# Adjacent columns for the stationary operands of the widest attention pattern, in a float32 decoder step on one core

## Chip, core and metric

The kernel runs on one core of a Trainium2 chip. The metric is the device time of one execution in microseconds; the kernel before takes 2777.18 us (median of three runs, 2773.69 to 2778.02).

## What is computed

One step of a decoder layer for a prompt of 2048 tokens and 8 sample tokens, width 1024, all in float32: a norm, one input projection to q, k, v and u, dilated attention on q, k, v (8 heads of 64) beside pooling on u, an output projection, an MLP with 4096 hidden features, a gated per-layer input and a final norm. The attention has three patterns, whose outputs are merged by their softmax denominators:

```python
DILATION_PATTERNS = ((128, 1), (512, 4), (2048, 16))
def _dilated_attn_prompt(q, k, v, window, dil):
    span = window // dil
    ...   # tokens are regrouped by residue modulo dil; in a class a query sees its own row and span rows before
    s = jnp.einsum('bdhnqe,bdhnke->bdhnqk', qb, kb).astype(jnp.float32) * ATTN_SCALE
    mask = (rel >= 0) & (rel <= span) & (key_idx >= 0)
    s = jnp.where(mask, s, NEG_INF)
    m = jnp.max(s, axis=-1, keepdims=True)
    p = jnp.exp(s - m)
    den = jnp.sum(p, axis=-1)
    ...
def _mixer_out(outs, lses, pooled, w_out):
    wts = jax.nn.softmax(jnp.stack(lses, axis=0), axis=0)
    attn = jnp.einsum('gbth,gbthe->bthe', wts, jnp.stack(outs, axis=0))
    ...
    return jnp.concatenate([attn, pooled], axis=-1) @ w_out
```

In the widest pattern (dilation 16) each of the 16 classes of the prompt has 128 tokens.

## The kernel before

Every float32 factor is split into a high and a low part, and each product is the sum of three passes on TensorE (line 190 records all of them). The projections run as groups of 24 passes with a stationary weight tile of 128x128 and 264 to 512 token columns moving. They are the work in front; the attention is a generator of steps in the background, which `Pace` mixes into the groups in proportion to the columns passed (lines 1526 and 1546). A scheduler with its own model of the chip then orders each engine's queue, so an engine's order can differ from the order in which the code is written. Each engine takes its queue in order.

The attention runs twice: `Att(0)` (called A here, from about 228 to 640 us) for the queries of tokens 0 to 1023, beside the second half of the input projection and `ple_mm`; `Att(1)` (B, about 640 to 1535 us) for the others, beside the output projection and most of the MLP of the first tokens. The rest, from 1535 us on, has the sample's last part, the other tokens' projections, MLP and gates, and no prompt attention.

Tokens are stored by their residue modulo 4: `khl[:, r, c]` is the key of token 4c + r (high part in rows 0 to 63, low part below), `qhh[:, r, c]` the query's high part twice, `ql` its low part. The class of dilation 16 is every fourth column of one `r`, written `s::4`, a step of 16 bytes. Per head there are three parts:

- `prep` and `prep_v` load and split keys, queries and values.
- `maxima` (line 761) gets an upper bound of the scores from single passes with the queries stationary; VectorE reduces them (line 771). For each `r` come two products of the middle pattern and four of the widest (line 789), with stationary `qhh[:, r, s::4]` and moving keys with the same step: 64 of them in A, 128 in B. For the first pattern GpSimd copies the queries of four blocks into the buffer `qn` (line 796, 128x512), two copies per head and half, and each serves four products (line 807).
- `out` runs `units` (line 865): scores, exponentials (ScalarE), masks (GpSimd), split (ScalarE, VectorE), and one unit later the products with the values (`pv`, `pv_wide`). Units of the middle pattern for r, r+1, then one of the widest for both (line 908), twice per head, then the first pattern. The widest unit has 16 score products: for each of 2 r and 4 s one with stationary keys `khl[:, r, s::4]` and moving `qhh`, and one with stationary `k1` (a copy of the keys' upper half by ScalarE, line 898, with a row of ones) and moving `ql`. Stationary are 64 columns in A, 128 in B; moving are 64.

For the first pattern GpSimd copies keys into natural order into the ring `nat` of two buffers (line 932), ScalarE into `k1` (line 933). After the last head of A, `prep_cat` loads the attention's output from DRAM, multiplies it by the reciprocal denominators and splits it (VectorE, ScalarE); the output projection (`out_proj`) uses the tiles of the pooling first and the tile of the last two heads last.

```python
                    mm(o, qhh[:, r, s::4], khl[:, r, s : 4 * self.kp : 4], True, True)
                ...
                    scores(ps[:kp, E * u : E * u + E], khl[:, r, s : 4 * kp : 4], k1s[u // 4][:, s : 4 * kp : 4],
                           qhh[:, r, s::4], ql[:, r, s::4])
```

Of the kernel before, what the change touches and what calls it, by code (L numbers as in the profile page):

```python
# [12 lines left out]
ALU = mybir.AluOpType  # L13
# [4 lines left out]
P = 128  # L18
D = 1024            # model width
KD = D // P         # feature tiles of the model width  # L20
SEQ = 2048
NS = 8              # sample tokens
# [7 lines left out]
WIN = 2048          # rows of the key/value cache  # L30

# Token 512 n + 4 i + r lies at position 512 n + 128 r + i; the sample's tokens lie behind the prompt's.
# Chunks of positions (first, length), each a PSUM bank's worth: phase 1 in two halves ...
IN_PART = [[(0, 512), (512, 512)], [(1024, 384), (1408, 384), (1792, 264)]]
# ... and the later phases in two parts, the first of which needs no token behind the 1,024th.
# [5 lines left out]
# On-chip memory in 4-byte columns: split operands (float32r), float32 data, two blocks that change hands.  # L41
GRAIN = 2 * LC        # a split operand of a chunk
COLS_R = 41 * GRAIN
COLS_MA = 3400
# [4 lines left out]
class Arena:  # L49
    """Columns of a few buffers, handed out by the oldest free stretch that is long enough."""  # L50
# [49 lines left out]
class Region(Arena):  # L100
    """Stretches of an arena, handed out in their turn."""
# [14 lines left out]
class Ring:  # L116
    """n buffers used in turn."""
# [31 lines left out]
def decoder_step(ctx: ExitStack, tc: tile.TileContext, I, O):  # L149
# [59 lines left out]
    class Pace:  # L209
        """Background steps spread over the work in front (columns through the tensor engine)."""  # L210
# [16 lines left out]
    def mix(a, na, b, nb, lead=1.0):  # L227
        """steps of a and b in proportion, those of b sooner by the factor lead"""
        i = j = 0
        while i < na or j < nb:  # L230
            if j * na >= i * nb * lead and i < na or j >= nb:
                i += 1
                next(a, None)
            else:
                j += 1
                next(b, None)
            yield
        drain(a)
        drain(b)

# [31 lines left out]
    # mask2: query i (partition) against the previous and the own block in natural order.  # L272
    # mask1: query (r, i') against (r, previous 32 | own 32), tokens 4 i' + r.
    # mask3: query 64 + i against the keys of its class.
# [23 lines left out]
    def TINY(cols, rows=P, key="", n=7, width=16):  # L298
        """a narrow buffer, in turn with those of the same key"""
# [7 lines left out]
    def newton(out, v, scr1, scr2):  # L307
        """out = v ** -0.5 with one Newton step behind the square root and the reciprocal."""
# [18 lines left out]
    def load_w(src, nk, nf=P, wr=None, ring=None):  # L327
        """src: DRAM [nk * 128, nf] -> its two parts, each [P, nk, nf]."""
# [12 lines left out]
    def group(ps, ln, ws, xs, hook=None):  # L341
        """ps = sum over k of w[k].T x[k], in the passes that float32 accuracy asks for."""
# [9 lines left out]
    class Acts:  # L352
        """Split activations [k][chunk] -> [P, 2, length]."""
# [37 lines left out]
    def pieces(pos, ln):  # L391
        """(first, end, group, offset in the group) of the stretch of positions"""
# [8 lines left out]
    def prep_x(hf, xa, rg, tp):  # L401
        """rg: rings xl, xraw, junk; tp: banks for the transposes"""
# [129 lines left out]
    def pool_state(rg, tp):  # L532
        """the sums over the buffered rows in the windows of the sample's tokens"""
# [24 lines left out]
    def group_done(ft, n, t, rg, tp):  # L558
        """t: one feature tile of q, k, v or u for the 512 positions of group n"""
# [23 lines left out]
    def in_proj(hf, xa, order, rg, mp, tp, hook, ws, first=None):  # L583
        """first: steps that come beside the first chunk's products of the first two tiles, and ahead of the other chunk's"""
# [1084 lines left out]
```

## Time and profile before

| | us |
|---|---|
| median of three runs | 2777.18 |
| span of the profiled execution, first to last instruction | 2772.4 |
| TensorE busy in it | 2701.8 |
| VectorE busy | 1525.1 |
| GpSimd busy | 978.0 |
| ScalarE busy | 805.3 |

The profile has no other time for the profiled execution than its span. Matmuls are pipelined: a matmul's duration in a row covers its fill and drain and overlaps its neighbours', so rows of TensorE are best read by the starts of runs. The granted clock is 1.00 at full speed and 0.50 at half.

### The profile page before, as it was taken

How to read it: one execution, taken by the hardware profiler on the slowest of the kernel's cores; microseconds unless marked ns; L12 is line 12 of the kernel's file. 1: busy time of each engine (PE TensorE's matmuls, PEld its weight loads, DVE VectorE, ACT ScalarE, POOL GpSimd, SP SyncE). 2: the span in 40 equal slices, each digit the busy share in tenths (PEclk: the TensorE clock that was granted, in tenths of full speed). 3: DMA queues.
4: the chain of work that ended last, by engine and by line, in shares of the span. 5: the costliest groups of instructions: out<-in, count | busy, mean ns of one | idle time of the engine just before them, and what ended most of it. 6: DMA issues, size and time to landing. Idle time of an engine off the chain costs nothing. (4 is left out here: it accounts for less than half of the span.)

```text
span 2772.4 us, 42788 instructions
## 1 busy us (share of the span) xinstructions
PE 2701.8 (97%) x15686; PEld 2588.0 (93%) x15686; DVE 1525.1 (55%) x3303; ACT 805.3 (29%) x1541; POOL 978.0 (35%) x1270
## 2 busy tenths in 40 slices
PE   8999999999989999999999999999999999999998
PEld 6788899988989999999999899899999999999997
DVE  6737866666586665755655766532332332322675
ACT  5211344452423133242332424411011011011354
POOL 2414634422375333332432734412122122122263
PEclk9999999999999999999999999999999999999999
DMA  7464345467153232332321554431111111111124
GB/s 245 136 176 124 90 109 135 105 211 195 39 160 107 72 87 69 103 101 71 91 71 50 156 155 145 130 115 42 43 39 39 39 40 44 39 39 39 52 83 148
DMA packets 386192, 272.50 MB, mean 98 GB/s; under 512 B 91722, under 2 KB 349461, under 8 KB 385973
## 3 DMA queue, kind: packets, MB, share of 16 engines
q1 hardware_dynamic: 385397, 269.68, 34.1%
q8 instruction: 123, 2.02, 0.3%
q14 instruction: 88, 0.72, 0.1%
q0 software_dynamic: 512, 0.07, 0.0%
q10 hardware_dynamic: 72, 0.02, 0.0%
HBM read 209.47 MB, written 60.30 MB: 97 GB/s over the span
## 5 line engine op out<-in xcount | busy, mean ns | idle before, releaser
L190 PE MATMUL bank<-mem_r 128*128 128x416 f32 (+10 forms) x13544 | 2501.4, 342 | 36.2 <-DVE mem_r L196 10.6
L190 PEld LDWEIGHTS bank<-mem_r 128*128 128x128 f32 (+3 forms) x13544 | 2359.5, 189 | 108.9 <-DVE mem_r L196 16.6
L199 POOL TENSOR_SCALAR mem_r<-mem_f 128x512 fp32r<-128x512 f32 (+1 forms) x444 | 323.8, 734 | 852.3 <-PE bank L190 729.5
L196 DVE TENSOR_TENSOR mem_r<-mem_f,mem_r 128x512 fp32r<-128x512 f32 (+4 forms) x568 | 432.6, 767 | 217.8 <-POOL mem_r L199 161.8
L196 DVE TENSOR_TENSOR mem_f<-bank,mem_f 128x416 f32<-128x416 f32 (+3 forms) x488 | 273.1, 566 | 257.8 <-PE bank L190 251.2
L196 DVE TENSOR_TENSOR mem_r<-mem_mb,mem_r 128x416 fp32r<-128x416 f32 (+6 forms) x236 | 172.9, 739 | 363.9 <-ACT mem_r L1310 310.4
L1307 ACT ACTIVATE mem_mb<-bank 128x392 f32<-128x392 f32 (+1 forms) x160 | 82.4, 515 | 799.3 <-PE bank L190 797.9
L196 POOL TENSOR_TENSOR mem_mb<-mem_mb 128x416 f32<-128x416 f32 (+1 forms) x140 | 142.4, 1017 | 314.8 <-ACT mem_mb L1307 290.9
L771 DVE CUSTOM_DVE_ANT_0 bank<-bank,mask 128x256 f32<-128x256 f32 (+3 forms) x504 | 158.5, 340 | 32.9 <-PE bank L190 29.0
L196 DVE TENSOR_TENSOR mem_ma<-bank,mem_ma 128x416 f32<-128x416 f32 (+2 forms) x104 | 63.5, 610 | 84.5 <-PE bank L190 71.5
L1310 ACT CAST mem_r<-mem_mb 128x416 fp32r<-128x416 f32 (+1 forms) x128 | 68.5, 535 | 139.6 <-POOL mem_mb L196 139.5
L834 POOL TENSOR_SCALAR_AFFINE_SELECT mem_ma<-mem_ma 128x256 f32<-128x256 f32 (+2 forms) x148 | 75.0, 527 | 93.7 <-ACT mem_ma L843 34.5
L190 PE MATMUL bank<-mem_mb,mem_r 128*128 128x512 f32 (+4 forms) x432 | 95.2, 340 | 7.9 <-DVE mem_ma L771 2.1
L190 PEld LDWEIGHTS bank<-mem_mb,mem_r 128*128 128x128 f32 (+1 forms) x432 | 75.0, 192 | 17.4 <-DVE mem_ma L771 2.7
L196 POOL TENSOR_TENSOR mem_f<-mem_f 128x416 f32<-128x416 f32 (+2 forms) x52 | 71.0, 1371 | 39.5 <-DMA mem_f<-in_cache_attn_kv_dram 22.6
L199 POOL TENSOR_SCALAR mem_r<-mem_r 128x512 fp32r<-128x512 f32 (+2 forms) x56 | 53.1, 966 | 82.5 <-PE bank L190 76.8
L196 DVE TENSOR_TENSOR mem_r<-mem_ma,mem_r 128x512 fp32r<-128x512 f32 (+4 forms) x88 | 68.9, 788 | 22.7 <-ACT mem_r L855 18.1
L771 DVE DVE_READ_ACCUMULATOR2_ANT mem_ma<- 128x1 f32 (+1 forms) x512 | 68.6, 134 | 0.0
L199 POOL TENSOR_SCALAR mem_r<-mem_mb 128x512 fp32r<-128x512 f32 (+2 forms) x48 | 48.6, 1023 | 49.9 <-PE bank L190 26.1
L834 POOL TENSOR_SCALAR_AFFINE_SELECT mem_mb<-mem_mb 128x256 f32<-128x256 f32 (+2 forms) x76 | 38.2, 521 | 77.2 <-ACT mem_mb L843 31.2
L196 POOL TENSOR_TENSOR mem_ma<-mem_ma 128x416 f32<-128x416 f32 (+1 forms) x41 | 51.5, 1263 | 39.0 <-DMA mem_ma<-h_s 15.7
L834 POOL TENSOR_SCALAR_AFFINE_SELECT mem_f<-mem_f 128x256 f32<-128x256 f32 (+2 forms) x72 | 34.1, 494 | 77.0 <-ACT mem_f L911 39.0
(249 smaller groups left out, 1773.0 us busy)
## 6 DMA issues: line engine op xcount, KB each, us to landing
mem_f<-in_w_up_dram SPq DMA_DIRECT2D x128, 256.0 KB
mem_f<-in_w_down_dram SPq DMA_DIRECT2D x128, 256.0 KB
mem_f<-in_w_in_dram SPq DMA_DIRECT2D x64, 256.0 KB
out_dram<-mem_f SPq DMA_DIRECT2D x55, 256.0 KB
mem_f<-in_cache_attn_kv_dram SPq DMA_DIRECT2D x48, 256.0 KB
mem_f<-in_w_ple_gate_dram SPq DMA_DIRECT2D x48, 256.0 KB
mem_f<-in_x_prompt_dram SPq DMA_DIRECT2D x64, 128.0 KB
xT_s<-mem_f SPq DMA_DIRECT2D x32, 256.0 KB
```

The costliest lines, as they stand in the source:

```text
L190: PE.matmul(out, l, r, start=start, stop=stop)
L196: eng.tensor_tensor(out, a, b, op=op)
L199: G.tensor_scalar(out, src, 1.0, 1.0, op0=ALU.mult, op1=ALU.mult)
L771: V.tensor_tensor_reduce(src, src, mask, 1.0, -3e38, ALU.add, ALU.max, mcol[: src.shape[0], col : col + 1])
L834: G.affine_select(out=p, in_=p, pattern=[[0, nblk], [sign, w]], compare_op=ALU.is_ge, fill=0.0, base=base, channel_multiplier=-sign)
L1307: S.activation(a, ps[:, :ln], AF.Relu)
L1310: S.copy(x[:, 0], sq)
```

## The change

In `maxima` the queries of a class r are copied by GpSimd, class s after class s, into a buffer of 256 columns, one copy per r, and the product takes 64 adjacent columns of it. The copies for the first pattern are cut into four of 256 columns per head and half. All eight copies of a head come from one iterator and are issued one ahead of their use, from a ring of three buffers in A and from the ring `nat` in B. In `units`, VectorE copies each r's keys into class order (`kc`), and ScalarE their upper half (`kc1`), beside the copy `k1` of before; the widest unit's 16 products take adjacent columns of these. In B `kc` takes the buffers of `nat`, and `kc1` a new ring. The queries that move in the scores and the keys that move in the maxima keep their step. The number of matmuls stays 15686.

```diff
@@ Att.__init__
+            if hf == 0:
+                rb["qn"] = Ring(M, 3, 256)
+            else:
+                rb["kc"] = Ring(M, 2, 512)
...
@@ maxima
+            qring = rb["qn" if hf == 0 else "nat"]
+            def by_class(r):
+                q = qring(256)
+                pcopy(q.rearrange("p (s c) -> p s c", s=4), f(qhh)[:, r].rearrange("p (c s) -> p s c", s=4))
+                return q
+            def by_block(nl, m):
+                q = qring(256)
+                pcopy(q.rearrange("p (b r i) -> p b r i", b=2, r=4),
+                      f(qhh).rearrange("p r (n m b i) -> p n m b r i", n=2, m=2, b=2)[:, nl, m])
+                return q
+            makes = iter([partial(by_class, r) for r in range(4)] + [partial(by_block, nl, m) for nl in range(2) for m in range(2)])
+            def ahead():
+                make = next(makes, None)
+                return make() if make else None
+            nxt = ahead()
             for r in range(4):
...
+                q, nxt = nxt, ahead()
                 ps = sp()
...
-                    mm(o, qhh[:, r, s::4], khl[:, r, s : 4 * self.kp : 4], True, True)
+                    mm(o, q[:, E * s : E * s + E], khl[:, r, s : 4 * self.kp : 4], True, True)
...
             for nl in range(2):
-                qn = rb["qn"]()
-                pcopy(qn.rearrange("p (b r i) -> p b r i", b=4, r=4),
-                      f(qhh).rearrange("p r (n b i) -> p n b r i", n=2, b=4)[:, nl])
                 for m in range(2):
+                    q, nxt = nxt, ahead()
...
-                        mm(o, qn[:, bb * P : bb * P + P], khl[:, :, lo : lo + w], True, True)
+                        mm(o, q[:, u * P : u * P + P], khl[:, :, lo : lo + w], True, True)
@@ units
+                pair = rb["nat"]() if hf == 0 else None
                 for r in (rp, rp + 1):
-                    k1 = rb["k1"](self.nk)
-                    k1s.append(k1)
-                    S.copy(k1[:E], f(khl[:E, r]))
+                    k1 = rb["k1"]()
+                    S.copy(k1[:E, : self.nk], f(khl[:E, r]))
+                    if hf == 0:
+                        kc, kc1 = pair[:, 256 * (r - rp) : 256 * (r - rp) + 256], k1[:, 256:]
+                    else:
+                        kc, kc1 = rb["nat"](), rb["kc"]()
+                    by16 = f(khl)[:, r].rearrange("p (c s) -> p s c", s=4)
+                    V.tensor_copy(kc.rearrange("p (s c) -> p s c", s=4), by16)
+                    S.copy(kc1[:E].rearrange("p (s c) -> p s c", s=4), by16[:E])
+                    kcs.append((kc, kc1))
...
-                    scores(ps[:kp, E * u : E * u + E], khl[:, r, s : 4 * kp : 4], k1s[u // 4][:, s : 4 * kp : 4],
-                           qhh[:, r, s::4], ql[:, r, s::4])
+                    kc, kc1 = (x[:, kp * s : kp * s + kp] for x in kcs[u // 4])
+                    scores(ps[:kp, E * u : E * u + E], kc, kc1, qhh[:, r, s::4], ql[:, r, s::4])
```

The memory plan follows: 24 columns go from one block to another, B's buffers lie at the upper end of their arena, 280 columns more than before, and the weights of the sample's attention stand in six small buffers in place of one.

In the queues this looks as follows. ScalarE, a widest unit of B with its two middle units (L843 / L868 the exponentials, L855 / L880 the split, L898 / L923 the copy `k1`, L911 / L945 the widest unit's exponentials, L1307, L1310 and L1344, L1347 the MLP), before:

```order
L1307 ACTIVATE mem_mb_6469<-bank_71 128x416
L843 ACTIVATE mem_ma_1831<-bank_74 128x512
L1310 CAST mem_r<-mem_f 128x416
L855 CAST mem_r<-mem_ma_1831 128x512
L843 ACTIVATE mem_mb_6469<-bank_75 128x512
L855 CAST mem_r<-mem_mb_6469 128x512
L1307 ACTIVATE mem_mb_6469<-bank_73 128x416
L898 CAST mem_r<-mem_r 64x512
L1310 CAST mem_r<-mem_mb_6469 128x416
L911 ACTIVATE mem_ma_1831<-bank_74 128x512
L898 CAST mem_r<-mem_r 64x512
```

and now:

```order
L868 ACTIVATE mem_ma_1831<-bank_74 128x512
L923 CAST mem_r<-mem_r 64x512
L1347 CAST mem_r<-mem_f 128x416
L880 CAST mem_r<-mem_ma_1831 128x512
L868 ACTIVATE mem_mb_6581<-bank_75 128x512
L923 CAST mem_r<-mem_r 64x512
L880 CAST mem_r<-mem_mb_6581 128x512
L1344 ACTIVATE mem_mb_6581<-bank_73 128x416
L931 CAST mem_r<-mem_r 64x512
L1347 CAST mem_r<-mem_mb_6581 128x416
L945 ACTIVATE mem_ma_1831<-bank_74 128x512
L931 CAST mem_r<-mem_r 64x512
```

The copies in class order (L931) for the second pair of a head stand around the first widest unit's exponentials, among the MLP's evictions.

GpSimd, near the last head of A (L834 / L859 the masks, L199 copies; those of queries are `mem_r` or `mem_mb` from the same memory), before:

```order
L834 AFFINE_SELECT mem_f<-mem_f 128x2x128
L834 AFFINE_SELECT mem_f<-mem_f 128x128
L834 AFFINE_SELECT mem_ma_1831<-mem_ma_1831 128x2x128
L834 AFFINE_SELECT mem_ma_1831<-mem_ma_1831 128x128
L199 TENSOR_SCALAR mem_r<-mem_r 128x512
L834 AFFINE_SELECT mem_f<-mem_f 64x512
L199 TENSOR_SCALAR mem_r<-mem_mb_69 128x4x128
```

and now:

```order
L199 TENSOR_SCALAR mem_r<-mem_r 128x256
L859 AFFINE_SELECT mem_ma_1831<-mem_ma_1831 64x512
L199 TENSOR_SCALAR mem_mb_69<-mem_r 128x256
L859 AFFINE_SELECT mem_f<-mem_f 128x2x128
L859 AFFINE_SELECT mem_f<-mem_f 128x128
L859 AFFINE_SELECT mem_ma_1831<-mem_ma_1831 128x2x128
L859 AFFINE_SELECT mem_ma_1831<-mem_ma_1831 128x128
L199 TENSOR_SCALAR mem_r<-mem_r 128x256
L199 TENSOR_SCALAR mem_mb_69<-mem_r 128x256
L199 TENSOR_SCALAR mem_r<-mem_r 128x256
```

A query copy of 512 columns has become several of 256, which stand between the masks of the head before.

TensorE, where A ends and the output projection (128x416) begins, before:

```order
L190 MATMUL bank_70<-mem_r 128x264 x6
L812 MATMUL bank_74<-ident_91,mem_ma_1831 16x128
L813 MATMUL bank_74<-ident_91,mem_ma_1831 16x64
L190 MATMUL bank_74<-mem_r 128x256
L190 MATMUL bank_71<-mem_r 128x264 x6
L190 MATMUL bank_70<-mem_r 128x416 x24
L190 MATMUL bank_71<-mem_r 128x416 x24
```

and now, from the last head's last product with values (65x128) on:

```order
L190 MATMUL bank_77<-mem_r 65x128
L190 MATMUL bank_74<-mem_r 128x256 x2
L190 MATMUL bank_71<-mem_r 128x264 x6
L190 MATMUL bank_75<-mem_r 64x128 x4
L190 MATMUL bank_70<-mem_r 128x416 x21
L190 MATMUL bank_77<-mem_r 64x128 x4
L190 MATMUL bank_76<-mem_r 128x256 x2
L190 MATMUL bank_71<-mem_r 128x416 x2
L190 MATMUL bank_73<-mem_r 128x416 x2
L190 MATMUL bank_71<-mem_r 128x416 x19
L190 MATMUL bank_73<-mem_r 128x416 x19
L190 MATMUL bank_75<-mem_r 64x128 x4
```

The first three groups of the projection are cut: 21 passes of each come first, then 12 products of B's maxima, of which the fence shows four, then three passes of each group, which need the last head's tile. Before, the maxima of B's first head (L812 is their end) stood ahead of the projection, and its groups were whole.

## Rows read from the trace of the kernel before

**Rows 1.** The page: span, and busy time of each engine

```profile
span 2772.4 us, 42788 instructions
PE 2701.8 (97%) x15686; PEld 2588.0 (93%) x15686; DVE 1525.1 (55%) x3303; ACT 805.3 (29%) x1541; POOL 978.0 (35%) x1270
```

**Rows 2.** By stretch: us, busy PE, PEld, DVE, ACT, POOL, granted clock, DMA

```profile
228.00:640.00 412.00, 400.57 (x2912) 377.68 (x2912) 287.98 (x918) 175.18 (x322) 178.81 (x269) 0.98 0.50 132
640.00:1535.00 895.00, 879.71 (x5179) 848.46 (x5178) 561.31 (x1286) 272.69 (x481) 354.29 (x469) 0.98 0.33 91
```

**Rows 3.** Waits of TensorE in A, then in B: us, times, longest

```profile
PE bank L190 <- POOL mem_r L199: 0.9, 1, 0.9
...
PE bank L190 <- DVE mem_r L196: 5.9, 6, 1.9
PE bank L190 <- DVE mem_f L196: 5.2, 4, 2.4
PE bank L190 <- POOL mem_r L199: 1.7, 3, 1.1
```

**Rows 4.** Groups of TensorE in 1313.70 to 1317.28: count, busy us, mean ns

```profile
L190 PE MATMUL bank<-mem_r 128*128 128x64 f32 x16 | 3.7, 395 | 0.0
```

**Rows 5.** Groups of TensorE in 303.46 to 305.28

```profile
L190 PE MATMUL bank<-mem_r 128*64 128x64 f32 x8 | 2.0, 290 | 0.0
L190 PE MATMUL bank<-mem_mb 128*64 128x64 f32 x8 | 1.9, 283 | 0.0
```

**Rows 6.** Timeline of TensorE around 754: start, us, then the run

```profile
754.02 1.11 PE L190 MATMUL bank<-mem_ma 128*65 128x64 f32 x16
754.93 0.43 PE L190 MATMUL bank<-mem_r 128*128 128x416 f32 x1
```

**Rows 7.** Timeline of TensorE around 149 (transposes)

```profile
148.46 0.71 PE L413 MATMUL bank<-ident,mem_f 128*128 128x128 f32 x5
149.01 0.60 PE L570 MATMUL bank<-ident,mem_f 128*128 128x128 f32 x4
149.44 0.49 PE L413 MATMUL bank<-ident,mem_f 128*128 128x128 f32 x3
149.69 0.48 PE L190 MATMUL bank<-mem_r 128*128 128x512 f32 x1
```

**Rows 8.** Groups of TensorE in 797.72 to 798.17

```profile
L190 PE MATMUL bank<-mem_r 128*64 128x128 f32 x4 | 0.6, 299 | 0.0
```

**Rows 9.** Timeline of TensorE around 236

```profile
236.00 0.56 PE L190 MATMUL bank<-mem_mb 128*64 128x64 f32 x4
236.39 0.86 PE L190 MATMUL bank<-mem_r 128*128 128x264 f32 x5
```

**Rows 10.** Stretches behind widest units, as rows 2 (the last one in A)

```profile
1188.85:1192.26 3.41, 3.41 (x31) 3.35 (x32) 0.59 (x1) 1.70 (x3) 0.99 (x2) 1.00 0.02 5
1317.30:1320.71 3.41, 3.41 (x11) 3.26 (x12) 0.31 (x1) 1.66 (x3) 1.96 (x3) 0.50 0.00 0
1399.31:1402.72 3.41, 3.41 (x17) 3.33 (x16) 0.00 (x0) 1.10 (x2) 0.66 (x1) 0.51 0.25 78
586.90:590.31 3.41, 3.41 (x13) 2.83 (x11) 2.11 (x4) 3.41 (x6) 0.65 (x1) 0.50 0.78 249
```

**Rows 11.** Groups of TensorE in 662.27 to 669.08 (one more reaches into it)

```profile
L190 PE MATMUL bank<-mem_r 128*128 128x416 f32 x37 | 7.2, 353 | 0.3 <-POOL mem_r L199 0.3
```

**Rows 12.** Groups of the whole span, by form: copies on GpSimd, ScalarE and VectorE

```profile
L199 POOL TENSOR_SCALAR mem_r<-mem_r 128x512 fp32r<-128x512 f32 x40 | 43.2, 1081 | 51.8 <-PE bank L190 46.1 <-ACT mem_r L737 3.1 <-DVE mem_r L196 2.6
...
L415 DVE COPY mem_f<-bank 128x512 f32<-128x512 f32 x32 | 21.8, 686 | 14.7 <-PE bank L413 8.2 <-DMA xT_s<-mem_f 5.5 <-PE bank L464 0.8
...
L933 ACT CAST mem_r<-mem_r 64x512 fp32r<-64x512 f32 x16 | 18.1, 1130 | 17.8 <-PE bank L190 17.8
```

**Rows 13.** Timelines of VectorE and of TensorE where A ends

```profile
636.14 0.68 DVE L196 TENSOR_TENSOR mem_ma<-bank,mem_ma 65x512 f32<-65x512 f32 x1
...
653.76 0.58 DVE L196 TENSOR_TENSOR mem_r<-mem_f,mem_r 128x416 fp32r<-128x416 f32 x1
...
662.01 4.20 PE L190 MATMUL bank<-mem_r 128*128 128x416 f32 x21 [0.30 <-POOL mem_r L199]
```

More of the change, by code (lines that the diff above doesn't have):

```diff
@@ L42 @@
 GRAIN = 2 * LC
-COLS_R = 41 * GRAIN
-COLS_MA = 3400
+COLS_R = 41 * GRAIN + 24
+COLS_MA = 3376
 COLS_MB = 4 * GRAIN
@@ L652, in __init__ @@
                 "vh": Ring(M, d, self.nb * (E + 1)), "vl": Ring(M, d, self.nb * E), "k1": Ring(M, 2, 512),
-                "ph": Ring(M, 2, 512), "pl": Ring(M, 2, 512), "nat": Ring(M, 2, 512), "qn": Ring(M, 1, 512),
+                "ph": Ring(M, 2, 512), "pl": Ring(M, 2, 512), "nat": Ring(M, 2, 512),
                 "m": Ring(F, 1, 32 + 192 + 384), "oa": Ring(F, 1, 1024), "v3": Ring(F, d, 16 * (E + 1)), "p": Ring(F, 2, 512), "ld": Ring(F, 3, 512),
@@ L656, in __init__ @@
             rb = self.rbufs
+            if hf == 0:
+                rb["qn"] = Ring(M, 3, 256)
+            else:
+                rb["kc"] = Ring(M, 2, 512)
             self.m = rb["m"]()
-            for b in rb["k1"].b:
+            for b in rb["k1"].b + (rb["kc"].b if hf else []):
                 G.memset(f(b.ap)[E:P, :], 0.0)
@@ L893, in units @@
                 cb = self.acc()
-                k1s = []
+                kcs = []
+                pair = rb["nat"]() if hf == 0 else None
                 for r in (rp, rp + 1):
-                    k1 = rb["k1"](self.nk)
-                    k1s.append(k1)
-                    S.copy(k1[:E], f(khl[:E, r]))
+                    k1 = rb["k1"]()
[8 more added lines that the diff above has]
+                    kcs.append((kc, kc1))
                     ps = self.sp()
@@ L1041, in sample_attn @@
             PE.transpose(pt[:, g * E : g * E + E], p[:, g * P : g * P + P], ident[:E, :E])
-        mem = R.alloc(384 + 1024, ("r",))
-        pw = mem.ap[:, :384].rearrange("p (g b a h) -> p g b a h", g=3, b=NS, a=2)
-        vh, vl = mem.ap[:, 384:896], mem.ap[:, 896:1408]
+        R.grain = 8
+        mem = [R.alloc(n, ("r",)) for n in 2 * [512] + 6 * [64]]
+        R.grain = GRAIN
+        vh, vl = mem[0].ap, mem[1].ap
+        pw = [m.ap.rearrange("p (b a h) -> p b a h", b=4, a=2) for m in mem[2:]]
         pt = pt[:, :192].rearrange("p (g b h) -> p g b h", g=3, b=NS)
-        for g in range(3):
-            V.tensor_copy(pw[:, g, :, 0], pt[:, g])
-            tt(V, pw[:, g, :, 1], pt[:, g], f(pw[:, g, :, 0]), ALU.subtract)
+        for j, w in enumerate(pw):
+            src = pt[:, j // 2, 4 * (j % 2) : 4 * (j % 2) + 4]
+            V.tensor_copy(w[:, :, 0], src)
+            tt(V, w[:, :, 1], src, f(w[:, :, 0]), ALU.subtract)
         own = C([2 * H, H], name="own")
@@ L1071, in sample_attn @@
                 tt(V, vl, vt, f(vh), ALU.subtract)
-                wb = pw[:, g, b].rearrange("p a h -> p (a h)")
+                wb = pw[2 * g + b // 4][:, b % 4].rearrange("p a h -> p (a h)")
                 mm(po[: 2 * H], wb, vh, g == 0, False)
@@ L1091, in sample_attn @@
         dma(att[:, SEQ:].rearrange("(k p) s -> p k s", p=P), o)
-        for x in (ring, scb, mem):
+        for x in (ring, scb, *mem):
             x.free()
@@ L1541, in decoder_step @@
     change_hands("mb", COLS_MB, R, F)
-    B = Att(1, Turns([bank[4], bank[5]]), att_acc, (14 * GRAIN, "r", False))
+    R.grain = 8
+    B = Att(1, Turns([bank[4], bank[5]]), att_acc, (14 * GRAIN + 280, "r", True))
+    R.grain = GRAIN
     bg = B.heads()
```

## The prediction

> **What bounds the kernel now.** I read the page first: TensorE is busy for 2701.8 of 2772.4 us, and no other engine passes 55% [rows 1]. The table by stretch then says where that holds: in the attention of the first half of the queries (228 to 640 us, "A") TensorE is busy for 400.57 of 412 us, in that of the second half (640 to 1535 us, "B") for 879.71 of 895 us, while VectorE, the next, stands at 288 of 412 and 561 of 895 [rows 2]. The list of waits agrees: TensorE waits for other engines for 10.8 us in A and 15.1 us in B, in pieces of 2.4 us at most; the largest pieces and all that GpSimd causes are in [rows 3]. So the end is set by how long TensorE needs for its own queue, in which attention's products stand between those of the projections. What shortens a product there comes off the end, if the operands are there when its turn comes.
>
> A duration in the trace covers fill and drain, so I take the price of a product from starts: the length of an undisturbed run, from its first start to that of the next form, over its products. In B the 16 score products of the widest pattern (stationary 128 keys with a step of four elements, 64 queries moving) take the whole of 1313.70 to 1317.28: 3.58 us, **224 ns** each [rows 4]. In A the same unit with 64 stationary keys takes 303.46 to 305.28, **114 ns** each [rows 5]. Products with adjacent stationary columns are cheaper at the same width or a larger one: 16 products with 65 stationary columns and 64 moving run from 754.02 to 754.93, **57 ns** each [rows 6], and 12 with 128 stationary and 128 moving columns from 148.46 to 149.69, **103 ns** each [rows 7]. 224 to 114 follows the number of stationary columns, not that of moving ones: four products of the maxima in B with 64 stationary and 128 moving columns, both with the step, take 797.72 to 798.17, **113 ns** each [rows 8], no more than with 64 moving.
>
> The Trainium skill (TensorE: Matmul & The Clock Gate, LDWEIGHTS (loading the stationary operand)) prices the load by its columns alone, P / 1.2 ns. By it 128 columns take an estimated 107 ns with any step, the first term below would be nothing, and the trace speaks against it: 224 and 103 ns for the same 128 columns.
>
> **The change part by part.** *Widest scores, B.* Eight heads with two units of 16 are 256 products. Their stationary copies now lie together, so 224 becomes 103 ns: 256 x 121 ns = **31.0 us** (29 if the stepped queries that still move cost a few ns, 32 at best).
> *Widest scores, A.* 256 products from 114 to 57 ns: **14.6 us**.
> *Maxima, A.* 128 products in fours: 236.00 to 236.39 is 97 ns each [rows 9]; to 57 ns that is **5.1 us**, and at 114 ns, the price in a long run, 7.3 us.
> *Maxima, B.* 128 products at 113 ns. Here 128 keys with the step still move, and no row shows such columns with a cheap stationary operand. From above they cost 113 ns, since that is the whole product [rows 8], and from below 57 ns. So 0 to 7.2 us; I take the middle, **3.6 us**.
> Sum on TensorE: **54.3 us**, from 48 to 61.
>
> *The clock.* The granted clock falls to 0.5 (1.2 GHz) for 3.41 us right behind eight of the sixteen such units of B, of which [rows 10] show the seventh and the last; behind the unit that ends at 1188.85 it stays at 1.00. What TensorE did before each fall was such a unit. In a fallen stretch it starts ten products of 416 columns; at full clock 36 of them take 662.27 to 669.08, 0.19 us each [rows 11], so ten are worth 1.9 us and a fall costs about 1.5 us. Eight cost 12 us. The same unit in A, at half the length, is hardly ever followed by a fall (one of 16, [rows 10]), and B's unit will be as short as that. I count six of eight as gone: **9 us** (0 to 12).
>
> *What is added.* For B, 32 VectorE copies of 128x512 (0.69 us, the row of a copy of that size) and 32 ScalarE copies of 64 rows (1.13 us, a rearranging copy of the same size); for A half-sized ones, 32 each, about 0.4 and 0.6 us by halving; on GpSimd 128 copies of 128x256 in place of 32 of 128x512, which cost 1.08 us, so 0.54 us each by halving [rows 12]. That is 35 us on VectorE, 55 on ScalarE and 35 on GpSimd, spread over 1300 us in which they idle for 450 us or more each [rows 2]. The work that hides them is TensorE's own queue; without that cover a copy costs TensorE its whole length. Copies of keys stand well ahead: in the order of ScalarE and VectorE the pair for a unit comes before or among products of the projections, and the closest pair I find has some dozen TensorE products in front of its first use. In B the second pair of a head rewrites the buffers of the first and so waits for its products; queued behind it on VectorE are the additions that empty the projections' banks, which have a run of 24 products (24 x 0.19 = 4.6 us) of room. The first near-pattern copy on GpSimd waits likewise, with weight splits behind it, which are made a whole run ahead.
> Thin are the copies of queries by block: 64 now, with often three to ten products of TensorE between copy and first use, and none in a few places. Before, the 32 such copies and the other GpSimd splits made TensorE wait four times, 2.6 us in all [rows 3]. Four times as many copies, half as long, most of those by class far ahead: **+6 us**, from 0 to 14.
>
> *Between A and B.* In the new order the last head of A ends later beside the projections. The kernel before needs 18.2 us from the last sum of that head (its start at 636.14) to the last split tile made of it (653.76 + 0.58), and the first product of the output projection starts at 662.01, so nothing waited [rows 13]. Now some 93 products stand between that head's last product and the first that reads its tile, 63 of them with 416 columns: about 63 x 0.19 + 30 x 0.11 = 15.3 us. It can wait 3 us, and a fall of the clock may follow: **+2 us** (0 to 5).
>
> All: -54.3 - 9 + 6 + 2 = **-55.3 us**. The profiled execution's span of 2772.4 becomes 2717.1; the median of the runs, 2777.18, lies 4.8 us above that span, so I add that and say **2722 us**.
>
> **The rivals.** *The load isn't what is slow.* If the price hung on something that the change leaves (the moving side, or the small product itself), TensorE would gain nothing and only the waits of 8 us would come: 2785 us, slower. For it: the queries of the scores still move with the step. Against it: 224 against 114 ns for the same 64 moving columns.
> *The moving step binds at half.* If a stepped moving column cost as much as a stepped stationary one, products with 64 of them would stay at 114 ns: A gains nothing, B's scores fall from 224 to 114 ns, 28 us, with 9 of the clock and 8 of waits 2748 us. Against it: 128 moving columns pass in 113 ns [rows 8], so 64 need at most 57. The Trainium skill (SBUF — State Buffer, Specifications (TRN2)) has such a rule, 16-byte lines that want two hits each, which a step of four float32 misses on either operand; on the stationary side the trace agrees (224 against 103 ns), on the moving side [rows 8] allow half of it at most.
> *GpSimd's copies come late.* Place: the 64 block copies in front of the first pattern's maxima. TensorE takes its queue in order, so all projections behind such a product wait too. From (54.3 + 9 - 2) / 64 = 0.96 us per copy on, the gain is gone; at 1.2 us, a whole old copy and a short queue, they cost 77 us and the end is at 2793 us, slower. For it: the short leads and GpSimd's foreground splits in the same queue. Against it: GpSimd is busy for 43% of A and 40% of B, and the copies of this kind before, with leads as short in places, cost 2.6 us in all.
> *Half is given back.* Waits in A, where VectorE is at 70%, and at the border add 25 us rather than 8, and most falls of the clock stay behind other causes: 2748 us.
>
> **How the numbers follow.** Forecast 0.80 (2722), load not the cause 0.04 (2785), moving step 0.04 (2748), GpSimd late 0.04 (2793), half given back 0.08 (2748). From the bounds of the terms the forecast's own case runs from -61 - 12 = -73 us (2704) to -48 + 19 = -29 us (2748); 2706 to 2746 leaves out about 2 in 10. Measurements of this kernel tell about 0.2%, 5.5 us, from no change. Faster by more than that: 0.92; within it, where a rival nearly cancels the gain: 0.03; slower: 0.05.
>
> **What would show it.** Runs of 16 score products in B of about 1.65 us instead of 3.58, in A of 0.9 instead of 1.82; fours of the maxima in A of about 0.25 us and in B between 0.23 and 0.45, which tells the price of stepped moving columns; two or three falls of the clock behind the units of B; TensorE's waits for GpSimd in A and B of 5 to 10 us instead of 2.6; the third stretch, behind 1535 us, as long as it was. It would be wrong if runs of score products stayed at their length, or if the waits in A and B grew by more than 30 us.

## The result, and the profile after

The changed kernel takes **2736.1 us** (median; 2732.9 to 2737.5) against 2777.2 us for the kernel before, a ratio of 0.985 with a 95% interval of 0.9835 to 0.9863: 41 us faster, where 55 were forecast. The time lies inside the range (2706 to 2746), the sign is right, and the mechanism is the one predicted; the gain fell 14 us short.

The profiled execution has a span of 2731.2 us, 41.2 less than before. First the page, to be read against [rows 1]: TensorE loses 50.7 us of busy time, VectorE and ScalarE gain 35 and 41 and GpSimd 52, and TensorE's share stays at 97%.

```profile
span 2731.2 us, 43094 instructions
PE 2651.1 (97%) x15686; PEld 2526.3 (92%) x15686; DVE 1559.9 (57%) x3373; ACT 846.6 (31%) x1605; POOL 1030.2 (38%) x1370
```

The next three fences are groups of TensorE by form inside stretches that begin with the first and end just before the first start behind a run. The first is a unit of 16 score products in B, from 1474.30 to 1476.00, the counterpart of [rows 4]; the second a unit in A, 303.60 to 304.55 ([rows 5]); the third four products of B's maxima, 810.10 to 810.55 ([rows 8]). The row of the next product, which reaches into each stretch, is left out.

```profile
L190 PE MATMUL bank<-mem_r 128*128 128x64 f32 x16 | 1.9, 278 | 0.0
```

```profile
L190 PE MATMUL bank<-mem_r 128*64 128x64 f32 x8 | 1.1, 241 | 0.0
L190 PE MATMUL bank<-mem_mb,mem_r 128*64 128x64 f32 x8 | 1.1, 238 | 0.0
```

```profile
L190 PE MATMUL bank<-mem_r 128*64 128x128 f32 x4 | 0.6, 293 | 0.0
```

By starts, B's unit fell from 3.58 to 1.70 us (106 ns a product), A's from 1.82 to 0.95 (60 ns), a four of A's maxima from 0.38 to 0.22, and a four of B's maxima from 0.45 to 0.45: nothing. Of 25 such uninterrupted fours, 24 take 0.45.

Then the stretches of [rows 2], with the same columns. They are fixed in time, so that the second now holds some 45 us of the stage behind the attention.

```profile
228.00:640.00 412.00, 393.91 (x2977) 366.42 (x2976) 295.59 (x942) 194.35 (x362) 207.41 (x321) 0.98 0.50 135
640.00:1535.00 895.00, 870.14 (x5312) 833.46 (x5311) 619.93 (x1375) 314.20 (x544) 414.71 (x546) 0.99 0.36 98
```

More products fit in, and TensorE is *less* busy in both: 393.91 for 400.57 us and 870.14 for 879.71. The list of TensorE's waits says for whom (us in total, times, longest; the three largest of A, then of B):

```profile
PE bank L190 <- ACT mem_r L880: 5.2, 4, 2.4
PE bank L190 <- DVE mem_r L196: 4.7, 8, 1.7
PE bank L190 <- POOL mem_r L199: 2.2, 2, 1.1
...
PE bank L190 <- DVE mem_f L196: 9.3, 11, 2.9
PE bank L190 <- DVE mem_r L196: 6.4, 8, 2.3
PE bank L190 <- POOL mem_r L199: 5.3, 4, 2.8
```

Against [rows 3], waits for GpSimd grew from 2.6 to 7.5 us, and those for ScalarE's split of the weights (L880) in A to 5.2 from the 0.5 of the kernel before, where the split is L855:

```profile
PE bank L190 <- ACT mem_r L855: 0.5, 1, 0.5
```

Those for VectorE's sums (mem_f) in B seem to grow from 5.2 to 9.3, but that is the fixed stretch. The last products of B's widest pattern with the values begin at 1481.6 us now and at 1526.3 before, and behind them both kernels have the same waits. The lists of 1481.6 to 1535 in the changed kernel and of 1526.3 to 1580 in the kernel before:

```profile
PE bank L190 <- DVE mem_f L196: 4.6, 4, 2.9
PE bank L190 <- ACT mem_mb L1344: 0.5, 1, 0.5
```

```profile
PE bank L190 <- DVE mem_f L196: 5.3, 4, 1.9
```

All rows of the two lists add up to 17.7 and 24.5 us, against 10.8 and 15.1. Without the 5.1 us behind 1481.6 that is 37.1 against 25.9: **11 us more** in the attention. The list of the whole span grew by 9, from 61 to 70 us.

Last the clock, in stretches as in [rows 10]. The unit that ends at 1291.95 us has no fall behind it; the second row is the stretch ahead of the fall at 860.3, the third that fall, the fourth the stretch ahead of the fall at 631.6:

```profile
1291.95:1295.36 3.41, 3.41 (x20) 3.38 (x20) 0.64 (x1) 0.84 (x2) 1.58 (x3) 1.00 0.06 19
...
856.90:860.30 3.40, 1.14 (x12) 0.79 (x10) 3.40 (x4) 1.79 (x4) 1.66 (x2) 1.00 0.02 5
860.30:863.71 3.41, 3.41 (x21) 3.35 (x20) 2.59 (x5) 2.23 (x4) 1.60 (x3) 0.50 0.29 84
...
627.00:631.60 4.60, 1.94 (x14) 1.23 (x12) 2.80 (x4) 4.60 (x9) 2.41 (x4) 1.00 0.92 231
```

The clock record has 9 falls in the whole span where it had 19. Right behind B's sixteen units there is none; the two shown follow stretches in which TensorE *waited* (busy for 1.14 of 3.40 and for 1.94 of 4.60 us).

**The sum, and what it leaves open.** Products by starts: 16 units of B by 1.88 us are 30.1, 16 of A by 0.87 are 13.9, 32 fours of A's maxima by 0.16 are 5.1, B's maxima 0: -49.1 us. Falls: against the prices at full clock, the starts in fallen stretches lose 22.4 us where they lost 32.8: -10.4 (an estimate, about -12 without the waits that lie inside these stretches). Together that is -59.5, and the span fell by 41.2: **18 us came back**. The listed waits of the attention are 11 of them. The other 7 lie between starts of products and in no row of the list, and their place is not shown.

### The profile page after: what moved, and what is told of

It is laid out like the page before. It is cut to its first block, busy times and chain, and to the rows that moved or that the text cites. A ratio compares the mean times of both kernels' runs of the same rounds, so it can differ in the third digit from the quotient of the medians.

```text
span 2731.2 us, 43094 instructions
## 1 busy us (share of the span) xinstructions
PE 2651.1 (97%) x15686; PEld 2526.3 (92%) x15686; DVE 1559.9 (57%) x3373; ACT 846.6 (31%) x1605; POOL 1030.2 (38%) x1370
## 5 line engine op out<-in xcount | busy, mean ns | idle before, releaser
L190 PE MATMUL bank<-mem_r 128*128 128x416 f32 (+11 forms) x13608 | 2454.0, 338 | 46.9 <-DVE mem_r L196 13.3
L190 PEld LDWEIGHTS bank<-mem_r 128*128 128x128 f32 (+2 forms) x13608 | 2307.9, 184 | 127.4 <-DVE mem_r L196 22.9
L199 POOL TENSOR_SCALAR mem_r<-mem_f 128x512 fp32r<-128x512 f32 (+1 forms) x444 | 325.2, 737 | 773.6 <-PE bank L190 689.1
L196 DVE TENSOR_TENSOR mem_r<-mem_f,mem_r 128x512 fp32r<-128x512 f32 (+3 forms) x568 | 435.5, 773 | 176.2 <-POOL mem_r L199 142.8
L1344 ACT ACTIVATE mem_mb<-bank 128x392 f32<-128x392 f32 (+1 forms) x160 | 82.2, 514 | 801.0 <-PE bank L190 801.0
L776 DVE CUSTOM_DVE_ANT_0 bank<-bank,mask 128x256 f32<-128x256 f32 (+3 forms) x504 | 159.8, 338 | 33.9 <-PE bank L190 30.1
L199 POOL TENSOR_SCALAR mem_r<-mem_r 128x256 fp32r<-128x256 f32 (+1 forms) x117 | 92.0, 798 | 92.2 <-PE bank L190 81.1
L1347 ACT CAST mem_r<-mem_mb 128x416 fp32r<-128x416 f32 (+1 forms) x128 | 68.5, 535 | 134.4 <-POOL mem_mb L196 134.4
L859 POOL TENSOR_SCALAR_AFFINE_SELECT mem_ma<-mem_ma 128x256 f32<-128x256 f32 (+2 forms) x148 | 72.0, 506 | 92.2 <-ACT mem_ma L871 49.3
L190 PE MATMUL bank<-mem_mb,mem_r 128*64 128x64 f32 (+4 forms) x494 | 100.7, 321 | 6.2 <-DVE mem_r L196 2.1
L199 POOL TENSOR_SCALAR mem_r<-mem_mb 128x512 fp32r<-128x512 f32 (+3 forms) x61 | 55.3, 913 | 79.4 <-PE bank L190 55.8
L196 DVE TENSOR_TENSOR mem_f<-mem_f,mem_ma 128x416 f32<-128x416 f32 (+1 forms) x64 | 46.9, 733 | 26.2 <-ACT mem_ma L1190 11.3
L859 POOL TENSOR_SCALAR_AFFINE_SELECT mem_mb<-mem_mb 128x256 f32<-128x256 f32 (+2 forms) x76 | 34.5, 474 | 57.9 <-ACT mem_mb L868 22.8
```

The lines of the kernel that those rows point to most:

```text
L190: PE.matmul(out, l, r, start=start, stop=stop)
L196: eng.tensor_tensor(out, a, b, op=op)
L199: G.tensor_scalar(out, src, 1.0, 1.0, op0=ALU.mult, op1=ALU.mult)
L776: V.tensor_tensor_reduce(src, src, mask, 1.0, -3e38, ALU.add, ALU.max, mcol[: src.shape[0], col : col + 1])
L859: G.affine_select(out=p, in_=p, pattern=[[0, nblk], [sign, w]], compare_op=ALU.is_ge, fill=0.0, base=base, channel_multiplier=-sign)
L1344: S.activation(a, ps[:, :ln], AF.Relu)
```

## The experiments

The theory: cheaper stationary operands and fewer falls, less the waits. Open were: why B's maxima gained nothing, what the falls hang on, and whether the 18 us that came back stem from the copies' work, from the copies' lateness, or from a faster TensorE alone. In all that follows, times are compared with runs of the kernel before on the same chip.

**1. The scores alone** (keys' copies as in the changed kernel, maxima as before; run twice).

```
- q = by_class(r); q = by_block(nl, m)          # 8 GpSimd copies of 128x256 a head and half
- mm(o, q[:, E*s : E*s+E], khl[:, r, s : 4*kp : 4])
+ qn = ring(); pcopy(...)                        # 2 of 128x512, as before (in B from the ring nat)
+ mm(o, qhh[:, r, s::4], khl[:, r, s : 4*kp : 4])
```

> The class-order key copies for the widest scores as in the changed kernel; the maxima as in the kernel before (stepped stationary queries, block copies of 512 columns). The theory (the gain is cheaper stationary operands in the scores plus the clock falls behind B's units of 16, minus waits) gives: products 512 x 60 to 121 ns, about -43 us, clock falls -10, waits +5 to +12, so 2725 to 2740 us against 2777 before. If the extra waits of the changed kernel come from the queries' copies on GpSimd, this kernel is at 2730 or below and its waits for GpSimd stay at 2.6 us in A and B together; if they come from the keys' copies on ScalarE and VectorE, it is at 2738 or above, slower than the changed kernel by about the 6 us that the maxima in A gain there. Clock falls: as few as in the changed kernel (about nine in the whole span).

Measured: 2726.9 us against 2779.0 (ratio 0.981, 0.9795 to 0.9828). Run again:

> The kernel with the scores alone (maxima as before) once more, as the measure for the next two on the same chip: 2727 us, ratio 0.981 to the kernel before.

Measured: 2729.3 against 2778.2 (0.9825, 0.9811 to 0.9839). So it is 50 us faster than before and **faster than the changed kernel**, although it gives up the 5 us of A's maxima. Its list of waits in B holds the same mem_f row and no row for GpSimd (0.6 us in the second run):

```profile
PE bank L190 <- DVE mem_f L196: 9.4, 7, 3.0
PE bank L190 <- DVE mem_r L196: 4.9, 4, 2.3
PE bank L190 <- ACT mem_r L861: 2.1, 3, 1.4
```

**2. The maxima alone.**

```
- S.copy(kc1...); V.tensor_copy(kc...); scores(..., kc, kc1, ...)
+ scores(..., khl[:, r, s : 4*kp : 4], k1[:, s : 4*kp : 4], ...)
```

> The maxima as in the changed kernel, the widest scores as in the kernel before (stepped stationary keys, no key copies). Theory: only A's 128 products of the maxima get cheaper (97 to 120 ns down to 60, 5 to 7 us); B's stay at 118 ns because 128 stepped columns move; the clock falls behind B's units of 16 stay (about eight, at 1.5 us each lost). So 2770 to 2777 us, with 0 to 5 us of waits for GpSimd given back. The rival that B's maxima gain too gives 2763 to 2767; the rival that the clock falls come from the maxima and not from the units of 16 gives about ten us less than the theory.

Measured: 2768.8 against 2779.0 (0.996, 0.9948 to 0.9976), 10 us faster and a little under the range expected. The fours of A account for 5; the profiled span (2769.1) is only 3.3 below that of before, so the rest of the 10 isn't found in the traces. All 128 copies of the queries are made here, and no cost of theirs shows. The parts don't add up: 50 and 10 apart, 41 together. The next runs ask where the 19 went.

**3. All copies made, those in class order not read.** Work is added here and nothing gets cheaper. (The copies by block, cut into four as in the changed kernel, are still read by the first pattern's maxima.)

```
- scores(..., kc, kc1, ...);  mm(o, q[:, E*s : E*s+E], ...)
+ scores(..., khl[:, r, s : 4*kp : 4], k1[:, s : 4*kp : 4], ...);  mm(o, qhh[:, r, s::4], ...)
```

> All copies are made as in the changed kernel, but the products of the widest pattern take the stepped operands of the kernel before. No product gets cheaper, and none waits for a class-order copy. What is measured is the price of the added work itself on VectorE, ScalarE and GpSimd. If the 19 us of added waits and small losses come from the engines' queues growing (ScalarE's and VectorE's copies standing ahead of the weights' split), it is at 2785 to 2795 us; if they come from products waiting for their copies, or only from TensorE running faster against unchanged other engines, it is within 3 us of 2777. Clock falls as before (19).

Measured: 2794.0 against 2779.0 (1.0053, 1.0038 to 1.0068), **15 us slower**. With the keys' copies alone made and unread (the maxima as before, their block copies in B in the ring `nat`):

> Only the keys' class-order copies are made (VectorE and ScalarE, 32 pairs in each half) and nothing reads them: the scores take the stepped keys, the maxima are as before. With all copies made and unused the time was 2794 us, 15 above the kernel before. If that is the queues of VectorE and ScalarE growing, this one is at 2789 to 2796; if it is the queries' copies on GpSimd, it is within 3 us of the kernel before, 2776 to 2783. In between, the two share it.

Measured: 2782.5 against 2778.2 (1.0017, 1.0006 to 1.0028), 4 us slower. So work on engines that no share of busy time makes critical costs 15 us: 4 for the keys' copies on ScalarE and VectorE, and by the difference 11 for the queries' copies on GpSimd beside them. The 11 are no price of GpSimd's copies by themselves, since in experiment 2 the same copies, without the keys', leave a kernel that is faster by more than its cheaper products explain. The two sets cost more together than apart. TensorE's lists with all copies made add up to 35 us in A and B, 9 more than before; the rows for GpSimd in A, then in B:

```profile
PE bank L190 <- POOL mem_r L199: 4.5, 2, 2.9
...
PE bank L190 <- POOL mem_r L199: 0.6, 1, 0.6
```

**4. B's maxima without their class-order copies** (A as in the changed kernel), beside the changed kernel on the same chip.

```
- mm(o, q[:, E*s : E*s+E], khl[...])             # both halves
+ mm(o, qhh[:, r, s::4] if hf else q[:, E*s : E*s+E], khl[...])   # copies of 512 columns in B
```

> The changed kernel without the class-order copies of the queries in B: there the maxima take stepped queries and block copies of 512 columns as before; A is as in the changed kernel. Theory: B's maxima gained nothing from their copies (pitch 118 ns in both), and the copies cost waits in B, 8.5 us of waits and small losses by the comparison with the kernel that has the scores alone (43.0 against 34.5 us). So the sum of products stays as in the changed kernel, and the time falls by 6 to 10 us to 2726 to 2730. Rival: the waits in B come from the keys' copies or from TensorE meeting the MLP's steps sooner, and the time stays within 3 us of the changed kernel's.

> The changed kernel once more, on the same chip as the next three. 2736 us again, a ratio of 0.985 to the kernel before. If the first comparison was off, and this one comes to 2727 to 2730, the difference to the kernel with the scores alone is no effect of the maxima.

Measured: 2731.6 (2728.2 to 2737.1) for the one, 2738.3 (2734.9 to 2739.9) for the changed kernel. The 6.7 us are the size expected; the ratios to the kernel before (0.9837, 0.9821 to 0.9854, and 0.9854, 0.9838 to 0.9870) overlap, so the size is less sure than the sign. B's maxima got nothing from 32 class copies and 32 block copies, and without them the kernel is faster. By which path, the traces don't settle. The list of waits in B has no row for GpSimd, where the changed kernel has 5.3 us (4.6 in the run beside this one), but its other rows are larger, and with 22.9 us in all it is no shorter than the 21.4 of that run:

```profile
PE bank L190 <- DVE mem_f L196: 10.3, 7, 3.3
PE bank L190 <- DVE mem_r L196: 6.7, 6, 2.3
PE bank L190 <- ACT mem_r L888: 2.1, 3, 1.4
PE bank L190 <- ACT mem_r L1273: 2.0, 1, 2.0
```

What did shrink between the two profiled executions is the loss in B's fallen stretches, from about 10 to 5 us by starts (an estimate, as above).

**5. What holds B's maxima at 112 ns.** The moving operand becomes 128 keys that lie side by side. These maxima are then over other keys than the class's: it is a probe, not a version to use.

```
- mm(o, q[...], khl[:, r, s : 4*kp : 4])
+ mm(o, q[...], khl[:, r, P*s : P*s + P] if hf else khl[:, r, s : 4*kp : 4])
```

> The changed kernel, in which the maxima of the widest pattern in B take 128 keys that lie side by side as the moving operand in place of the class's keys (so these maxima are over other keys than the reference's). Theory: the moving columns' step is what holds those products at 118 ns, so they fall to about 60 ns and TensorE's sum by 128 x 58 ns = 7.4 us: 2727 to 2732 us against 2736. Rival: the stationary load or the write into the bank holds them, the pitch stays at 110 to 120 ns and the time at 2736. A third: the pitch falls but VectorE's reductions bind, pitch 60 ns and time 2736.

Measured: 2731.0 against 2779.0 (0.983, 0.9814 to 0.9845), 5 to 7 us below the changed kernel's two medians, with intervals that overlap. The starts are clearer. A four from 913.15 to 913.39, by form:

```profile
L190 PE MATMUL bank<-mem_r 128*64 128x128 f32 x4 | 0.4, 223 | 0.0
```

That is 0.24 us for the four instead of 0.45: 60 ns each, and 128 x 52 ns is 6.7 us. The step of the *moving* columns held them. A moving column with the step of four elements costs 112 / 128 = 0.88 ns, a stationary one 224 / 128 = 1.75 ns; the dearer operand sets the product's price (113 ns with the step on both, [rows 8]). The Trainium skill (SBUF — State Buffer, Specifications (TRN2)) has a rule that bears on both, 16-byte lines that want two hits each; the trace agrees on either operand, at half the price for the moving one.

**6. The halves apart.**

```
- scores(..., kc, kc1, ...)
+ if hf == 0:                                   # in the other kernel: if hf == 1
+     scores(..., khl[:, r, s : 4*kp : 4], k1[:, s : 4*kp : 4], ...)
+ else:
+     scores(..., kc, kc1, ...)
  # the maxima as before in both
```

> The class-order copies of the keys in B alone; A's scores and all maxima as before. Theory: products of B 256 x 121 to 112 ns = 28 to 31 us, B's clock falls about 10 us, less 2 to 5 us of waits, so 2738 to 2746 us against 2777. If the clock falls are set by something else than the stepped units of 16, they stay (19 in the span) and the time is 2747 to 2752.

> The class-order copies of the keys in A alone; B's scores and all maxima as before. Theory: 256 products from 120 to 60 ns = 15 us, less 5 to 8 us of waits and small losses in A (43.7 against 36.9 us in the kernel with all scores), so 2767 to 2773 us; the clock falls behind B's units stay.

Measured: B alone 2740.7 against 2780.1 (0.986, 0.9848 to 0.9880), 39 us faster; A alone 2761.9 (0.994, 0.9926 to 0.9961), 18 us faster and 5 below the range expected. Together they make 58, against 52 and 49 when both are in. The stretch from 640 to 1535 us shows the granted clock (the third number from the end), 0.97 with A alone:

```profile
640.00:1535.00 895.00, 887.34 (x5196) 858.53 (x5195) 565.12 (x1282) 275.34 (x486) 357.97 (x478) 0.97 0.34 91
```

and 0.99 with B alone, where TensorE is also less busy:

```profile
640.00:1535.00 895.00, 871.66 (x5371) 839.22 (x5370) 619.00 (x1382) 315.86 (x550) 380.34 (x494) 0.99 0.37 100
```

By starts (an estimate, as above), the falls in B lost 18 us before, 25 with A alone, 27 with the maxima alone and 21 to 22 with copies unread; in the kernels with B's scores on copies they lost 4 to 11. In the five traces whose units in B keep the step, a fall begins behind 8 to 15 of the 16 units; in the nine whose units are adjacent, behind one of 144, and there a wait of TensorE lies in between. Most falls hang on B's stepped units, and go with them.

**7. The 128-row copy on another engine**, from the scores alone.

```
- V.tensor_copy(kc..., by16)
+ pcopy(kc..., by16)        # GpSimd; in the other kernel S.copy(kc..., by16), ScalarE
```

> As the one before it, with the 128-row copy of the keys on GpSimd (about 1.1 us each) in place of VectorE (0.67 us each). VectorE loses 21 us of work in B, where TensorE waits 9.4 us for its additions into the sums. If VectorE's queue is what holds TensorE, 3 to 6 us faster than the one before it (2721 to 2724); if GpSimd's masks come later by it, 0 to 8 us slower, with TensorE's waits for ScalarE's split of the weights growing from 2.1 us.

> The same copy on ScalarE, which is busy for 318 of 895 us in B, three copies in a row there. VectorE's relief as in the one before; the exponentials and splits of the weights queue 1.1 us longer on ScalarE. 2721 to 2725 if VectorE's queue is what holds TensorE and ScalarE has room; 2728 to 2740 if the split's lateness binds, as its 5.2 us of waits in A in the changed kernel suggest.

Measured beside the second run of the scores alone, 2729.3 (2728.3 to 2730.2): on GpSimd 2735.4 (2733.9 to 2737.1), 6 us slower; on ScalarE 2725.2 (2723.9 to 2731.3), 4 us faster, with intervals that overlap (0.9795 to 0.9823 against 0.9811 to 0.9839). TensorE's waits in B, of the version with GpSimd:

```profile
PE bank L190 <- DVE mem_f L196: 10.7, 9, 3.0
PE bank L190 <- DVE mem_r L196: 8.7, 6, 4.5
PE bank L190 <- POOL mem_r L199: 2.5, 1, 2.5
```

and of the one with ScalarE:

```profile
PE bank L190 <- DVE mem_f L196: 10.6, 8, 3.3
PE bank L190 <- DVE mem_r L196: 2.8, 4, 1.0
```

For the sums the theory that VectorE's queue holds TensorE fell: without the copies on VectorE the waits for them (mem_f) stay, at 10.6. That row had not grown in the first place: 4 to 5 us of it lie behind B's last widest products, as in the result, and ahead of them there are 5.2 us in the kernel before, 5.0 with the scores alone and 6.2 with ScalarE's copy. ScalarE's time, at the edge of the range named for the theory, doesn't decide. What fell with ScalarE's copy is mem_r, VectorE's splits, from 4.9 to 2.8; with GpSimd's it rose to 8.7, although the copies had left VectorE there too. VectorE makes the low part of a weight from the high part that GpSimd makes (L199): on the page of the kernel before, most of VectorE's idle time ahead of those splits ends with L199.

```profile
L196 DVE TENSOR_TENSOR mem_r<-mem_f,mem_r 128x512 fp32r<-128x512 f32 (+4 forms) x568 | 432.6, 767 | 217.8 <-POOL mem_r L199 161.8
```

So a late GpSimd can show as a late VectorE. VectorE's own operations also take longer beside GpSimd's copies (last section), and the runs don't separate the two. By the medians the scores alone with ScalarE's copy are the fastest version of the study, 53 us under the kernel before.

## Why the prediction was right, and what was mis-sized

- *Widest scores, B and A*: forecast 31.0 and 14.6, measured 30.1 and 13.9. The reading of [rows 4, 5] against [rows 6, 7] held: the step of the stationary columns made the products slow. The rival "load isn't what is slow" is out, and so is "the moving step binds at half" with its price, since 64 moving columns with the step pass in 60 ns; at 128 the same step does bind (B's maxima, below).
- *Maxima, A*: 5.1 forecast, 5.1 by starts. On top of the scores this gain isn't seen: 2731.6 with A's maxima copied, 2727 to 2729 without.
- *Maxima, B*: 3.6 forecast, 0 measured. This term failed in its value, not in its bound. [rows 8] already showed a product with both steps at 113 ns, and I took the middle between "all of it is the load" and "none of it". Experiment 5 shows that the moving side alone costs 112, so nothing could come off.
- *The clock*: -9 forecast, -10.4 by the estimate above, for the reason named, and better than I counted: no unit of B is followed by a fall, where two or three were expected. Part is given back by new falls behind waits.
- *Waits*: +8 forecast (6 for copies, 2 at the border); 18 came back, 11 of them in the list of the attention. This is the term that was mis-sized. The waits that name GpSimd were sized well: 4.9 us more, where "four times as many copies, half as long" had given 6. What I had put at nothing is the split of the attention's weights on ScalarE: 5.8 us more (5.2 in A and 1.1 in B, for 0.5), 2.4 of it at the border. The largest wait for it away from the border begins on GpSimd. The copy of 3.98 us at 317.81 us (last section) and the next one stand ahead of a mask; ScalarE's split waits for the mask, and TensorE for the split. GpSimd's, ScalarE's and TensorE's timelines (start, us):

```profile
321.76 1.47 POOL L199 TENSOR_SCALAR mem_mb<-mem_mb 128x256 fp32r<-128x256 f32 x1
...
323.79 1.21 POOL L859 TENSOR_SCALAR_AFFINE_SELECT mem_ma<-mem_ma 128x256 f32<-128x256 f32 x2
...
325.03 0.62 ACT L880 CAST mem_r<-mem_ma 128x512 fp32r<-128x512 f32 x1 [3.45 <-POOL mem_ma L859]
...
325.70 0.45 PE L190 MATMUL bank<-mem_r 128*65 128x256 f32 x2 [1.17 <-ACT mem_r L880]
```

  The copies are also longer than "half as long". By groups of the whole span, those of 128x256 whose buffers have one name:

```profile
L199 POOL TENSOR_SCALAR mem_r<-mem_r 128x256 fp32r<-128x256 f32 x85 | 65.8, 780 | 78.0 <-PE bank L190 66.8 <-ACT mem_r L742 6.3 <-ACT mem_mb L1344 3.2
```

  That is 780 ns, not the 540 that halving [rows 12] gave. Over all 128, taken in the order of the queue, the copies by block have a mean of 0.52 us, as forecast, and those in class order 1.09. On the page GpSimd has 979.0 us of work with the scores alone (the row below) and 1030.2 in the changed kernel, 51 us more where I had 35.

```profile
PE 2651.8 (97%) x15686; PEld 2533.9 (93%) x15686; DVE 1559.0 (57%) x3373; ACT 847.9 (31%) x1605; POOL 979.0 (36%) x1274
```

- *"Copies of keys stand well ahead"* failed where A ends. ScalarE's timeline (start, us) shows two key copies of B's first unit, `k1` and the new one in class order (L931, 1.10 us), in the queue ahead of the split of A's last weights, for which TensorE waits 2.4 us; the fall at 631.6 follows. ScalarE has no idle time there (4.60 of 4.60 us in the stretch above), so the new copy is a part of the delay and not all of it.

```profile
628.34 0.62 ACT L923 CAST mem_r<-mem_r 64x512 fp32r<-64x512 f32 x1
628.86 1.10 ACT L931 CAST mem_r<-mem_r 64x512 fp32r<-64x512 f32 x1
629.86 0.62 ACT L880 CAST mem_r<-mem_ma 128x512 fp32r<-128x512 f32 x1
```

- *"GpSimd's copies come late"* was a rival at 4%. It didn't decide the sign, but it named the right engine: 11 us in experiment 3 (beside the keys' copies), 7 in experiment 4, 6 in experiment 7.
- *The third stretch* was to stay as it was: from B's last widest product to the last product 1243.3 us before, 1246.2 after.

Not settled: why the two parts lose 19 us together. Most of it can be had without a faster TensorE: made and not read, the keys' copies cost 4 us and both sets 15, and the queries' copies alone show no cost (experiment 2), so 11 us or more come from both sets at once, each difference being sure to some 4 us. Experiment 4 gives 7 us to the queries' copies in B. Which of the things that the two sets share does it (the queues with the masks and splits, the ring `nat` in B, the slowing of VectorE and GpSimd by each other in the last section) no run separates.

## What to carry to other kernels

Before paying for a copy that makes one operand of a product adjacent, look at the step of the other: the dearer operand sets the price, and a copy that leaves it in place buys nothing. An engine at 38% of the span is not free when its queue also makes what the bottleneck needs next; to price added work, make it and leave it unread, and do so beside the other work that is added, since here two sets of copies cost more together than apart. Compare stretches that hold the same work: a row of waits seemed to double only because the next stage had moved into the stretch. A stretch of slow products can cost more than its length, through the clock that falls behind it, and the cure of the one is the cure of the other.

## What the hardware showed that I had not expected

GpSimd's class copies have no fixed length. Two of the same 128x256 in GpSimd's timeline of the changed kernel (start, us):

```profile
516.24 0.64 POOL L199 TENSOR_SCALAR mem_mb<-mem_mb 128x256 fp32r<-128x256 f32 x1
...
317.81 3.98 POOL L199 TENSOR_SCALAR mem_r<-mem_mb 128x256 fp32r<-128x256 f32 x1
```

and VectorE's timeline beside the second:

```profile
317.42 1.47 DVE L196 TENSOR_TENSOR mem_r<-mem_f,mem_mb 64x512 fp32r<-64x512 f32 x2
...
319.02 1.65 DVE L196 TENSOR_TENSOR mem_r<-mem_f,mem_r 128x512 fp32r<-128x512 f32 x2
320.60 0.69 DVE L196 TENSOR_TENSOR mem_f<-mem_f 128x527 f32<-128x527 f32 x1
```

Of the 64 class copies, seven have no two-operand operation of VectorE beside them, and six of those take 0.64 to 0.66 us; the median of all is 1.07, and the one at 317.81, beside such operations along nearly its whole length, takes 3.98. It goes the other way as well: the versions of experiment 7 give VectorE the same 3309 instructions, and with 64 copies more on GpSimd these take 18.6 us longer. The page of GpSimd's version, then of ScalarE's:

```profile
PE 2652.4 (97%) x15686; PEld 2535.0 (93%) x15686; DVE 1540.5 (56%) x3309; ACT 846.7 (31%) x1605; POOL 1032.0 (38%) x1338
```

```profile
PE 2656.8 (97%) x15686; PEld 2540.1 (93%) x15686; DVE 1521.9 (56%) x3309; ACT 897.5 (33%) x1669; POOL 965.4 (35%) x1274
```

The Trainium skill (SBUF — State Buffer, Terms) says that VectorE and GpSimd share a pair of ports and that the loser stands still for the other's whole instruction. The trace agrees in that each engine takes longer beside the other; that the loser stands still for a whole instruction no row here shows by itself. A copy's price taken by halving a mean of [rows 12] could not hold that.
